# Where the low halves of four operands of the recurrence's branch are made

## The chip, the cores and the metric

One core of a Trainium2 chip runs the kernel. It has five engines that work beside each other: TensorE (PE in the profile, with its weight loads as PEld), VectorE (DVE), ScalarE (ACT), GpSimd (POOL) and SyncE (SP), and 16 DMA engines that serve queues which SP, ACT and POOL issue to. The metric is the device time of one execution in microseconds; lower is better. Everything is in float32.

## The reference

One decoder layer, sequence 1024, model width 1024. Cut to what matters:

```python
h    = rmsnorm(x, pre_g)
proj = h @ w_in           # z_ssm, xBC, dt, q, k, v, f, z_att, g_ssm, g_att
y_ssm = norm(ssd(conv_silu(xBC), softplus(dt)) * silu(z_ssm))   # the recurrence's branch
y_att = forgetting_attention(q, k, v, cumsum(log_sigmoid(f))) * silu(z_att)
p_ssm = y_ssm @ w_branch_ssm
p_att = y_att @ w_branch_att
merged = sigmoid(g_ssm) * p_ssm + sigmoid(g_att) * p_att
out = x + rmsnorm(merged @ w_out, post_g)
```

The recurrence is a chunked state-space scan of 16 heads; attention has 16 heads of 64 channels, is causal, and goes in blocks of 128 queries.

## The kernel before, in words

**Products in two pieces.** A float32 product is made from float32r matmuls: each operand is split into a high piece (a rounded copy, ACT) and a low piece (what the copy left over, DVE), and high·high, high·low and low·high are added in PSUM.

**Seven products for eight.** Every big matrix product (1024 x 1024 by two column blocks of 128) is a `Pair`, done by a Strassen-Winograd scheme with seven products of half size. The moving operand is cut into four blocks B11, B12, B21, B22 of 512 x 512, each four row tiles j = 0..3 of 128 x 512. The seven products need B11, B21, -B22 and the differences T1 = B12 - B11, T2 = B22 - T1, T3 = T2 - B11, T4 = T2 - B21. Each of the seven has a place in SBUF, a high tile and a low tile: x0 is B11, x1 is B21, x2 is -B22, x3 is T1, x4 is -T2, x5 is T3, x6 is T4 (so the profile's `x5l` is the low tile of T3, `x5h` the high one).

**The stream.** `Stream` lists the steps of all 47 pairs in order; a step is 12 matmuls of 128 x 512, done in two halves. TensorE's instructions stand in the order of the program, whatever the scheduler does with the other engines; instructions wrapped in `pin` keep the program's order on their engine too. All others are ordered by a planner that models the time. The first 24 pairs make the projections, then come 11 gate pairs (`late`), four for `w_branch_ssm` (their operand set is `ops_s`), four for `w_branch_att` (`ops_a`) and four for `w_out` (`ops_w`).

**Attention between the halves.** Attention runs over 8 pairs of heads with 6 groups each (m = 0..47). In each m the scores' matmuls go out, then some halves of the stream ("ahead"), then the transposes of the exponentials, then some more halves ("behind"), and the product with the values in the next m. DVE takes the scores with the bias and their minimum (L1505), ACT the exponentials (L1509), ACT or DVE the transposed blocks (L1548, L1546). POOL adds the causal mask to the bias tile (L1373).

**The operand set of the recurrence's branch.** `y_ssm` lies in DRAM as `ys_dram`. From the first m of attention on, `ops_s.differences` is worked off as a list (`stream.line`), one entry for each half of the stream: SP loads blocks (L227, L206), POOL subtracts (L211), POOL's queue stores T1..T4 in DRAM (L193, tensor `t_s`). The tile `x` has one buffer, the second operand is a `th` tile. `th` is a pool of four buffers of 128 x 512 (`small`), which serves the gates' results (L413 to L419, L629), `rb` (L1438), `st` (L1431) and more.

**The placing.** When the last gate pair has done its last step with an operand, that operand's tiles are opened for `ops_s`. `some`, called once in each half, issues loads (`fetch`, L263) of up to two row tiles and, some halves later, splits up to two: ACT makes the high tile from the raw one (L275, L278), DVE the low one (L276, L279). `ops_w` has been made otherwise in three operands: their low pieces are made early with the differences, kept in DRAM and loaded into the low tile (L261), the raw block is loaded into the high tile (L263), and only ACT's copy in place is left (L269).

Of the kernel before, what the change touches and what calls it, by code (L numbers as in the profile page):

```python
# [8 lines left out]
F32 = mybir.dt.float32  # L9
F32R = mybir.dt.float32r  # L10
BF16 = mybir.dt.bfloat16
AF = mybir.ActivationFunctionType
ALU = mybir.AluOpType
# [3 lines left out]
P = 128  # L17
# [3 lines left out]
KH = NK // 2  # L21
NT = T // P
HALF = 512
# [63 lines left out]
def hybrid_layer(ctx: ExitStack, tc, a, out):  # L87

    nc = tc.nc
# [43 lines left out]
    def pin(op):  # L133
        return tc.keep_in_program_order(op)

    def small(name="th"):
        return gp.tile([P, HALF], F32, tag="th", name=name)
# [21 lines left out]
    class Operands:  # L159
# [9 lines left out]
        def __init__(self, name, src, there=lambda k, h: True, order=lambda op: op, queue=nc.gpsimd):  # L169
            self.src, self.there, self.order, self.queue = src, there, order, queue  # L170
            self.copy = src
            self.tiles, self.left, self.made, self.at, self.step = {}, {}, set(), {}, 0
            self.lows = {}
            self.dram = {n: tc.dram_tile([KH, P, HALF], F32, name=f"{n}_{name}") for n in self.LESS}

        def __getitem__(self, name):
# [7 lines left out]
            return self.dram[name][j]  # L184

        def ready(self, name, j):
            if name in self.BLOCKS:
                r, h = self.BLOCKS[name]
                return self.there(KH * r + j, h)
            return (name, j) in self.made  # L190

        def store(self, name, j, t, cols=slice(0, HALF)):
            pin(self.queue.dma_start(self.dram[name][j][:, cols], t))  # L193
            if cols.stop == HALF:
                self.made.add((name, j))

        def differences(self, j, x, other, cols=slice(0, HALF), room=2, third=None):

            state = {}

            def fetch(name):
                state["y"] = other()
                self.order(nc.sync.dma_start(state["y"], self.block(name, j)[:, cols]))  # L206

            def less(name, out_, a_, b_):
                def go():
                    t = {"x": state["x"], "y": state["y"]}  # L210
                    pin(nc.gpsimd.tensor_tensor(t[out_], t[a_], t[b_], ALU.subtract))  # L211
                    state["out"] = name, t[out_]

                return go

            def keep(following=None):
                def go():
                    name, t = state["out"]
                    self.store(name, j, t, cols)
                    if following:  # L220
                        fetch(following)

                return go

            def start():
                state["x"] = x()
                self.order(nc.sync.dma_start(state["x"], self.block("b12", j)[:, cols]))  # L227
                fetch("b11")

            def low(name):  # L230
                if third is None:
                    return

                def go():
                    t, y = third(), state["x" if name == "t4" else "y"]
                    if name == "b22":
                        pin(nc.scalar.activation(t.bitcast(F32R), y, AF.Copy, scale=-1.0))
                        pin(nc.vector.scalar_tensor_tensor(t.bitcast(F32R), y, -1.0, t, ALU.mult, ALU.subtract))
                    else:
                        pin(nc.scalar.activation(t.bitcast(F32R), y, AF.Copy))  # L240
                        pin(nc.vector.tensor_tensor(t.bitcast(F32R), y, t, ALU.subtract))
                    state["low"] = t

                yield go
                yield lambda: pin(self.queue.dma_start(self.lows[name][j][:, cols], state["low"]))

            wait = (None,) * room
            yield from (start, *wait, less("t1", "x", "x", "y"), keep("b22"), *wait)
            yield from (*low("b22"), less("t2", "x", "y", "x"), keep("b11"), *wait)
            yield from (less("t3", "y", "x", "y"), keep(), *low("t3"), *wait[1:], lambda: fetch("b21"), *wait)  # L250
            yield from (less("t4", "x", "x", "y"), keep(), *low("t4"))
# [5 lines left out]
        def fetch(self, name, j):  # L257
            block = name.strip("-")
            raw = self.tiles[name][block not in self.lows][:, j, :].bitcast(F32)
            if block in self.lows:  # L260
                nc.sync.dma_start(self.tiles[name][1][:, j, :].bitcast(F32), self.lows[block][j])  # L261
            r, c = self.BLOCKS.get(block, (0, 0))
            nc.sync.dma_start(raw, self.copy(KH * r + j, c) if block in self.BLOCKS else self.dram[block][j])  # L263

        def split(self, name, j, raw=None):
            h, l = (t[:, j, :] for t in self.tiles[name])
            if name.strip("-") in self.lows:

                pin(nc.scalar.activation(h, h.bitcast(F32), AF.Copy, scale=-1.0 if name[0] == "-" else 1.0))  # L269
                self.left[name].remove(j)  # L270
                return
            if raw is None:
                raw = l.bitcast(F32)
            if name[0] == "-":
                pin(nc.scalar.activation(h, raw, AF.Copy, scale=-1.0))  # L275
                pin(nc.vector.scalar_tensor_tensor(l, raw, -1.0, h, ALU.mult, ALU.subtract))  # L276
            else:
                pin(nc.scalar.activation(h, raw, AF.Copy))  # L278
                pin(nc.vector.tensor_tensor(l, raw, h, ALU.subtract))  # L279
            self.left[name].remove(j)  # L280
# [39 lines left out]
    class Pair:  # L320
# [78 lines left out]
        def keep(self, ps):  # L399
            s = wp.tile([P, HALF], F32, tag="s", bufs=3, name="s")  # L400
            with tc.high_priority():
                nc.scalar.activation(s, ps, AF.Copy)  # L402
            return s
# [57 lines left out]
    class Stream:  # L461
# [73 lines left out]
        def half(self):  # L535
            if self.run is None:
                if self.at == len(self.steps):
                    return False
                p, which = self.steps[self.at]
                if which == 7 and p.ops is ops_a and "merged" not in fin:  # L540
                    return False
                if p.ops is ops_a and not all(p.ops.ready(OPERAND[which].strip("-"), j) for j in range(KH)):
                    return False
                self.ahead(False)
                for ops in self.building:
                    ops.some(OPERAND[which])
                if self.at + 1 < len(self.steps):
                    after, then = self.steps[self.at + 1]
                    after.begin(then, after.sums + (after is p and which in (5, 7)), True)
                self.run = p.do(which)  # L550
                next(self.run)
            else:
                for _ in self.run:
                    pass
                self.run = None
                p, which = self.steps[self.at]
                if p in self.following:
                    ops = self.following[p]
                    if ops not in self.building:
                        self.building.append(ops)  # L560
                    ops.open(OPERAND[which])
                self.ahead(True)
                self.at += 1
            for ops in self.building:
                if self.held is None:
                    ops.some()
                else:
                    self.held.append(ops)
            for chores in (self.chores, self.line):
                if chores:  # L570
                    chore = chores.pop(0)
                    if chore:
                        chore()
            self.count += 1
            for w in self.waiting:
                w[0] -= 1
            for w in [w for w in self.waiting if w[0] <= 0]:
                self.waiting.remove(w)
                w[1]()
            return True  # L580
# [572 lines left out]
    ops_s = Operands("s", lambda k, h: ys_dram[k, :, half(h)])  # L1153
    ops_a = Operands("a", lambda k, h: ya_dram[k, :, half(h)], lambda k, h: (k, h) in attended)
    ops_w = Operands("w", lambda k, h: a["wo"][k * P : (k + 1) * P, half(h)], order=pin, queue=nc.sync)
    ops_w.lows = {n: tc.dram_tile([KH, P, HALF], F32, name=f"{n}_low") for n in ("t3", "t4", "b22")}
    ops_w.copy = lambda k, h: wo_dram[k, :, half(h)]

# [634 lines left out]
```

## Time and profile before

| what | us |
|---|---|
| median of 3 runs | 1278.0 |
| lowest and highest run | 1276.09, 1281.77 |
| profiled execution, its own time | 1273.87 |
| its span, first to last instruction | 1272.2 |
| busy: PE, DVE, ACT, POOL | 1246.1, 1012.9, 794.3, 319.3 |

The profile's times count from the first instruction of the span. `ops_s`'s differences are made from 683 to 898 us and placed from 908 to 976 us; attention goes on to about 1120 us. A view by stretches gives each engine's busy time within a stretch, with the number of its instructions in brackets. A row of a tile's view has shortest/median/longest duration in ns and the first and last start. A row of the waits has the total in us, the number of waits and the longest.

### The profile page before, as it was taken

How to read it: one execution, taken by the hardware profiler on the slowest of the kernel's cores; microseconds unless marked ns; L12 is line 12 of the kernel's file. 1: busy time of each engine (PE TensorE's matmuls, PEld its weight loads, DVE VectorE, ACT ScalarE, POOL GpSimd, SP SyncE). 2: the span in 40 equal slices, each digit the busy share in tenths (PEclk: the TensorE clock that was granted, in tenths of full speed). 3: DMA queues.
4: the chain of work that ended last, by engine and by line, in shares of the span. 5: the costliest groups of instructions: out<-in, count | busy, mean ns of one | idle time of the engine just before them, and what ended most of it. 6: DMA issues, size and time to landing. Idle time of an engine off the chain costs nothing.

```text
span 1272.2 us, 20822 instructions
## 1 busy us (share of the span) xinstructions
PE 1246.1 (98%) x6926; PEld 982.3 (77%) x6926; DVE 1012.9 (80%) x1994; ACT 794.3 (62%) x1737; POOL 319.3 (25%) x322
## 2 busy tenths in 40 slices
PE   5999999999999999999999999999999999999997
PEld 3678888888888888888887777777777777778886
DVE  7988886988888978997767676767789767886975
ACT  7745665556665765566555666666687666844753
POOL 4000440013400241115102124223112212356062
PEclk9999999999999999999999999999999999999999
DMA  8232452545436533744447576666687657766933
GB/s 300 69 120 76 146 162 88 191 152 182 138 101 215 175 127 117 219 146 140 142 149 252 162 228 212 217 214 218 232 286 263 224 184 249 249 221 199 364 110 105
DMA packets 152236, 233.56 MB, mean 184 GB/s; under 512 B 15201, under 2 KB 60737, under 8 KB 152129
## 3 DMA queue, kind: packets, MB, share of 16 engines
q1 hardware_dynamic: 136064, 196.08, 47.7%
q10 hardware_dynamic: 10560, 18.06, 3.8%
q0 software_dynamic: 5504, 18.09, 3.7%
q8 instruction: 54, 0.88, 0.3%
q14 instruction: 54, 0.43, 0.1%
HBM read 162.99 MB, written 72.34 MB: 185 GB/s over the span
## 4 chain that ended last, share of the span: by engine, by line
PE 86%; DMA 4%; DVE 4%; ACT 4%; issue 1%; SPq 0%; POOL 0%; DVEq 0%; ACTq 0%; POOLq 0%
PE pb L128 36%; PE pc L128 21%; PE pd L128 7%; PE av L128 5%; PE pt L131 5%; PE s L128 5%; PE yps L128 2%; PE st L128 1%; ACT ex L1509 1%; DMA xt<-in_x 1%; PE tr L131 1%; PE tr_v L131 1%; DMA v<-v_dram 1%; PE df L128 1%; DVE wop L350 1%
## 5 line engine op out<-in xcount | busy, mean ns | idle before, releaser
L350 DVE TENSOR_TENSOR wop<-sum,wop 128x512 fp32r<-128x512 f32 x180 | 140.2, 780 | 53.6 <-ACT wop L349 52.6
L349 ACT ACTIVATE wop<-sum 128x512 fp32r<-128x512 f32 x180 | 112.5, 626 | 109.0 <-DVE sum L355 52.4
L1509 ACT ACTIVATE ex<-ex,nm 128x512 f32<-128x512 f32 (+1 forms) x192 | 116.2, 606 | 71.9 <-DVE nm L1505 71.6
L402 ACT ACTIVATE s<-pb 128x512 f32<-128x512 f32 x144 | 85.3, 593 | 98.2 <-PE pb L128 96.2
L128 PE MATMUL pb<-x0h,wop 128*128 128x512 f32 x384 | 131.5, 399 | 0.0
L128 PE MATMUL pb<-x6h,wop 128*128 128x512 f32 x384 | 129.5, 395 | 1.3 <-ACT s L402 1.3
L128 PE MATMUL pb<-x5h,wop 128*128 128x512 f32 x384 | 130.1, 396 | 0.7 <-ACT s L402 0.7
L350 DVE TENSOR_TENSOR wop<-raw,wop 128x512 fp32r<-128x512 f32 x144 | 105.4, 733 | 31.8 <-ACT wop L349 31.5
L128 PE MATMUL pc<-x3h,wop 128*128 128x512 f32 x384 | 129.8, 396 | 0.5 <-DVE ot L419 0.4
L128 PE MATMUL pc<-x2h,wop 128*128 128x512 f32 x384 | 130.2, 397 | 0.0
L128 PE MATMUL pb<-x4h,wop 128*128 128x512 f32 x384 | 129.1, 395 | 0.0
L1505 DVE CUSTOM_DVE_ANT_0 ex<-s,fb 128x512 f32<-128x512 f32 (+1 forms) x192 | 96.8, 552 | 20.0 <-PE s L128 14.8
L349 ACT ACTIVATE wop<-raw 128x512 fp32r<-128x512 f32 x144 | 89.7, 623 | 14.7 <-PE pd L128 6.1
L128 PE MATMUL pd<-x1h,wop 128*128 128x512 f32 x288 | 96.3, 394 | 0.0
L128 PEld LDWEIGHTS pb<-x6h,wop 128*128 128x128 f32 x384 | 72.1, 188 | 18.6 <-issue 2.0
L128 PEld LDWEIGHTS pb<-x5h,wop 128*128 128x128 f32 x384 | 72.1, 188 | 18.4 <-issue 2.0
L128 PEld LDWEIGHTS pb<-x0h,wop 128*128 128x128 f32 x384 | 72.6, 189 | 17.6 <-issue 2.9
L128 PEld LDWEIGHTS pc<-x3h,wop 128*128 128x128 f32 x384 | 72.1, 188 | 17.7 <-issue 1.5
L128 PEld LDWEIGHTS pc<-x2h,wop 128*128 128x128 f32 x384 | 72.1, 188 | 17.4 <-issue 2.4
L128 PEld LDWEIGHTS pb<-x4h,wop 128*128 128x128 f32 x384 | 72.1, 188 | 16.7 <-issue 1.9
L211 POOL TENSOR_TENSOR wd<-wd 128x256 f32<-128x256 f32 x32 | 32.4, 1011 | 205.0 <-DMA wd<-in_wo 135.0
L131 PE MATMUL pt<-ident,ex 128*128 128x128 f32 x576 | 75.1, 273 | 2.0 <-ACT ex L1509 1.4
(318 smaller groups left out, 2993.6 us busy)
## 6 DMA issues: line engine op xcount, KB each, us to landing
raw<-in_wu SPq DMA_DIRECT2D x128, 256.0 KB
csb<-cs_dram SPq DMA_DIRECT2D x32, 256.0 KB
q<-q_dram SPq DMA_DIRECT2D x32, 256.0 KB
k<-k_dram SPq DMA_DIRECT2D x16, 512.0 KB
fb<-f_dram SPq DMA_DIRECT2D x16, 512.0 KB
rb<-st_dram SPq DMA_DIRECT2D x48, 128.0 KB
wd<-in_wo SPq DMA_DIRECT2D x40, 128.0 KB
xt<-in_x SPq DMA_DIRECT2D x8, 512.0 KB
```

The source lines that it names most:

```text
L128: return tc.keep_in_program_order(nc.tensor.matmul(*args, **kw))
L131: return tc.keep_in_program_order(nc.tensor.transpose(out_, in_, idn))
L211: pin(nc.gpsimd.tensor_tensor(t[out_], t[a_], t[b_], ALU.subtract))
L349: nc.scalar.activation(op[:, 0], src, AF.Copy)
L350: nc.vector.tensor_tensor(op[:, 1], src, op[:, 0], ALU.subtract)
L402: nc.scalar.activation(s, ps, AF.Copy)
L1505: nc.vector.tensor_tensor_reduce(o, s[e][:, 0:w], fb[hp, h][:, e, 0:w], 1.0, 3.0e38, ALU.add, ALU.min, nm)
L1509: pin(nc.scalar.activation(o, o, AF.Exp, scale=-1.0, bias=nm, accum_out=hd.at(hd.sm, i, h, e)))
```

## The change

Four of the seven operands of `ops_s`, namely T1, T3, T4 and B22, get their low pieces while the differences are made. `lower` takes a `th` buffer, lets ACT write the high piece into it and DVE turn it into the low piece (for B22 with the sign turned), and stores it on POOL's queue in a DRAM tensor of its own. ACT's and DVE's instruction and the store are pinned. The list of `differences` has 20 entries for a row tile where it had 19: `part` makes the piece one half after the stored difference, and T2's difference comes in the same half as B22's piece, behind it. An operand of these four counts as made only when its low piece has been issued. In the placing, `fetch` then loads two blocks for a row tile in place of one, and `split` is ACT's copy in place. T2, B11 and B21 stay as they are, and so do `ops_a` and `ops_w`.

```diff
             self.tiles, self.left, self.made, self.at, self.step = {}, {}, set(), {}, 0
-            self.lows = {}
+            self.lows, self.late = {}, ()
...
         def ready(self, name, j):
-            if name in self.BLOCKS:
+            if name in self.BLOCKS and name not in self.late:
...
-            if cols.stop == HALF:
+            if cols.stop == HALF and name not in self.late:
                 self.made.add((name, j))
+
+        def lower(self, name, j, t):
+
+            s = small()
+            pin(nc.scalar.activation(s.bitcast(F32R), t, AF.Copy, scale=-1.0 if name == "b22" else 1.0))
+            if name == "b22":
+                pin(nc.vector.scalar_tensor_tensor(s.bitcast(F32R), t, -1.0, s, ALU.mult, ALU.subtract))
+            else:
+                pin(nc.vector.tensor_tensor(s.bitcast(F32R), t, s, ALU.subtract))
+            pin(self.queue.dma_start(self.lows[name][j], s))
+            self.made.add((name, j))
...
             wait = (None,) * room
+            if self.late:
+                part = lambda name, t: lambda: self.lower(name, j, state[t])
+                behind = lambda *fns: lambda: [fn() for fn in fns]
+                yield from (start, *wait, less("t1", "x", "x", "y"), keep("b22"), part("t1", "x"), None)
+                yield from (behind(part("b22", "y"), less("t2", "x", "y", "x")), keep("b11"), *wait)
+                yield from (less("t3", "y", "x", "y"), keep(), part("t3", "y"), lambda: fetch("b21"), *wait)
+                yield from (less("t4", "x", "x", "y"), keep(), part("t4", "x"))
+                return
             yield from (start, *wait, less("t1", "x", "x", "y"), keep("b22"), *wait)
...
         def split(self, name, j, raw=None):
             h, l = (t[:, j, :] for t in self.tiles[name])
-            if name.strip("-") in self.lows:
+            if raw is None and name.strip("-") in self.lows:
...
+    ops_s.late = ("t1", "t3", "t4", "b22")
+    ops_s.lows = {n: tc.dram_tile([KH, P, HALF], F32, name=f"{n}_low_s") for n in ops_s.late}
```

## The prediction

> **What bounds the kernel now.** I read the page first, then the view by stretches over attention, then the waits in two stretches, and last the rows of the tiles that the change touches.
>
> ```profile
> span 1272.2 us, 20822 instructions
> ...
> PE 1246.1 (98%) x6926; PEld 982.3 (77%) x6926; DVE 1012.9 (80%) x1994; ACT 794.3 (62%) x1737; POOL 319.3 (25%) x322
> ...
> PE 86%; DMA 4%; DVE 4%; ACT 4%; issue 1%; SPq 0%; POOL 0%; DVEq 0%; ACTq 0%; POOLq 0%
> ```
>
> TensorE is busy for 98% of the span and makes 86% of the chain that ended last. The change adds and removes no matmul and leaves their order alone. So time can only come from stretches in which TensorE stands or is stretched, and only be lost by making it stand. Here are the two stretches that matter, the making of the differences (683 to 910 us) and the placing (910 to 980), and then pieces of 20 us.
>
> ```profile
> core 0: us, PE busy (x) PEld busy (x) DVE busy (x) ACT busy (x) POOL busy (x), PEclk, DMA share, GB/s
> 683.00:910.00 227.00, 226.34 (x1532) 172.13 (x1530) 160.85 (x433) 148.71 (x378) 62.87 (x77) 1.00 0.62 203
> 910.00:980.00 70.00, 68.24 (x445) 49.92 (x444) 60.35 (x151) 54.34 (x133) 12.51 (x19) 1.00 0.82 281
> ```
>
> ```profile
> 860.00:880.00 20.00, 20.00 (x133) 15.30 (x132) 15.99 (x38) 13.38 (x32) 8.97 (x12) 1.00 0.67 212
> ...
> 900.00:920.00 20.00, 20.00 (x141) 14.93 (x137) 14.64 (x42) 13.38 (x33) 1.85 (x3) 1.00 0.72 247
> 920.00:940.00 20.00, 19.90 (x143) 15.12 (x137) 17.17 (x48) 15.26 (x39) 4.58 (x7) 1.00 0.79 271
> 940.00:960.00 20.00, 18.73 (x113) 12.95 (x109) 18.63 (x41) 16.71 (x41) 2.71 (x5) 1.00 0.90 312
> 960.00:980.00 20.00, 19.62 (x128) 14.61 (x125) 18.25 (x46) 15.88 (x40) 4.68 (x6) 1.00 0.69 228
> 980.00:1000.00 20.00, 20.00 (x141) 15.47 (x140) 14.48 (x44) 12.51 (x35) 6.57 (x8) 1.00 0.57 181
> ```
>
> The granted clock is 1.00 throughout. TensorE stands 0.66 us in the whole making of the differences. In the placing it stands 1.76 us, 1.27 of them from 940 to 960, where DVE is busy for 18.63 of 20 us and ACT for 16.71. The waits of that piece name the chain, scores to DVE's minimum to ACT's exponential to the transposes:
>
> ```profile
> ACT ex L1509 <- DVE nm L1505: 3.3, 3, 1.4
> ...
> PEld pt L131 <- ACT ex L1509: 1.2, 1, 1.2
> ...
> PE pt L131 <- ACT ex L1509: 0.9, 1, 0.9
> ```
>
> **What the change takes away.** Sixteen DVE subtractions leave the placing (four operands, four row tiles). In the crowded piece DVE's timeline has six of them, among the minima that the exponentials wait for:
>
> ```profile
> 950.08 0.68 DVE L279 TENSOR_TENSOR x5l<-x5l,x5h 128x512 fp32r<-128x512 f32 x1
> ...
> 951.63 0.68 DVE L279 TENSOR_TENSOR x5l<-x5l,x5h 128x512 fp32r<-128x512 f32 x1
> ...
> 955.61 1.28 DVE L279 TENSOR_TENSOR x5l<-x5l,x5h 128x512 fp32r<-128x512 f32 x2
> 956.81 1.29 DVE L279 TENSOR_TENSOR x3l<-x3l,x3h 128x512 fp32r<-128x512 f32 x2
> ```
>
> Six at 0.68 us are 4.1 us: DVE's load from 940 to 960 falls from 18.63 to 14.5, that of 980 to 1000, where TensorE does not stand at all. ACT keeps its copies, so 16.71 of 20 stays there. The least that can be gained, if DVE was the cause, is the visible standing, 1.76 us. The most comes from the weight loads: the pieces 860, 900, 920 and 980 hold 15.2 us of them on average, 940 to 960 is short of that by 2.25 and 960 to 980 by 0.6, together 2.85 us of loads or 2.85 / 15.2 x 20 = 3.75 us of work (part of it may be another mixture of matmuls). I take **-2.5**, near the middle, because ACT's share stays.
>
> **What it adds beside attention.** Per piece one ACT copy, one DVE subtraction, one store on POOL's queue; sixteen of each. These are the rows for them:
>
> ```profile
> L278 ACT ACTIVATE x5h<-x5l x7: 615/621/622, 946.5 to 1103.8; 128x512 fp32r<-128x512 f32 x7
> ```
>
> ```profile
> L350 DVE TENSOR_TENSOR wop<-raw,wop 128x512 fp32r<-128x512 f32 x23 | 18.5, 804 | 13.7 <-ACT wop L349 13.7
> ```
>
> ```profile
> L193 POOL DMA_DIRECT2D t_s<-x x12: 542/559/559, 691.1 to 898.4; - x12
> ...
> DMA to landing us min/median/max: 2.3/3.0/8.1
> ```
>
> ACT: 16 x 0.62 = 9.9 us. DVE: the same shape with both sources in SBUF has a mean of 804 ns between 683 and 910 us, so 16 x 0.80 = 12.9 us. POOL: 16 x 0.56 = 9.0 us. Over 227 us that is +1.1 us of DVE and +0.9 of ACT in each 20. The fullest piece shown, 860 to 880, goes to 17.1 for DVE and 14.3 for ACT. The nearest row is 920 to 940, with 17.17 and 15.26: TensorE stood 0.10 us there. So the load alone costs from 0 to 0.1 in each of 11 pieces, 1.1 us, and the average piece is well below that row: **+0.5**.
>
> The 0.80 us deserve a look, since the same subtraction takes 0.68 in the placing. POOL's own differences stretch as well:
>
> ```profile
> L1373 POOL TENSOR_TENSOR fb<-fb,far 64x256 f32<-64x256 f32 x34 | 25.5, 749 | 54.1 <-DVE nm L1505 39.2 <-ACT ex L1509 13.5
> L211 POOL TENSOR_TENSOR x<-x,th 128x512 f32<-128x512 f32 x8 | 10.7, 1343 | 9.4 <-DMA th<-ys_dram 9.0
> ...
> L211 POOL TENSOR_TENSOR th<-x,th 128x512 f32<-128x512 f32 x4 | 6.4, 1589 | 0.3
> ```
>
> The Trainium skill, page "SBUF — State Buffer", section "SBUF: two separate sides", says that a DVE instruction with two sources in SBUF and a GpSimd instruction that reads SBUF exclude each other for a whole instruction. That speaks against this change, since it moves two-source subtractions to where POOL is 28% busy (62.87 of 227) from where it is 18% busy (12.51 of 70). The trace agrees in kind, by 804 ns against 0.68 us; by the rule each collision would cost DVE up to a whole POOL instruction, 1.6 us, and 28% of 16 would be 7.2 us of DVE where the means give 1.9. DVE would then gain 1.6 us in each 20 in place of 1.1, and the sum would be some 0.5 us higher.
>
> **The waits that it adds.** ACT's copy is pinned: it waits for POOL's difference, and the exponentials of the following scores stand behind it on ACT. It comes two halves after the difference. A half lasts 2.92 us, from the first T1 to the last T4, 71 entries of the list apart:
>
> ```profile
> L211 POOL TENSOR_TENSOR x<-x,th x8: 1278/1287/1718, 689.6 to 896.8; 128x512 f32<-128x512 f32 x8
> ```
>
> (896.8 - 689.6) / 71 = 2.92, and the difference takes 1.3, so it is done as a rule. DVE's subtraction waits at most ACT's 0.6 us. The store waits on POOL for DVE; behind it stand the next difference, the masks (L1373) and attention's stores. POOL is idle for 164 of the 227 us, and TensorE has no wait there that names it: 0 at best; at worst 16 x 1.4 (a copy and a subtraction) = 22 us, if every mask came that much late. I take 0, by that absence.
>
> The copy also needs one of the four `th` buffers. Their shortage shows already, in four waits that name the last user of such a buffer and not a source:
>
> ```profile
> DVE th L419 <- DMA gs_dram<-th: 1.7, 1, 1.7
> ...
> ACT th L644 <- DMA za_dram<-th: 1.0, 1, 1.0
> ...
> ACT st L1431 <- POOL x L211: 0.9, 1, 0.9
> ...
> DVE th L419 <- DMA st_dram<-st: 0.8, 1, 0.8
> ```
>
> A piece holds its buffer through 0.62 + 0.80 + 0.56 and a landing of 3.0, 5 us; sixteen hold one for 80 us of 227 x 4. That is 9% more use, and if it doubles the waits, 4.4 us more of them stand on DVE and ACT. Of the standing of ACT and DVE little reaches TensorE:
>
> ```profile
> ACT ex L1509 <- DVE nm L1505: 33.2, 29, 3.0
> ...
> PEld s L128 <- ACT p L1548: 4.9, 14, 0.4
> ...
> PEld pt L131 <- ACT ex L1509: 1.4, 3, 0.5
> ...
> PE pt L131 <- ACT ex L1509: 0.5, 2, 0.3
> ```
>
> ACT's exponentials wait 33.2 us and TensorE for them 1.9. Bounds 0 and 4.4; I take **+1.5**, a third, since a pinned copy holds the exponentials themselves.
>
> **The placing, with more transfers.** Sixteen more loads of 128 x 512 x 4 bytes = 256 KB, at SP's 0.43 us each (row below) 6.8 us of SP, and 4.2 MB. From 910 to 980 the chip moves 281 GB/s x 70 us = 19.7 MB at a share of 0.82; 23.9 MB would be 341 GB/s, a share of 1.00 (281 / 0.82 = 343). It fits with nothing to spare. The loads come early: T4's raw tiles are asked for from 950.7 and split from 963.2.
>
> ```profile
> L278 ACT ACTIVATE x6h<-x6l x7: 615/617/625, 963.2 to 1124.0; 128x512 fp32r<-128x512 f32 x7
> ...
> L263 SPq DMA_DIRECT2D x6l<-t_s x4: 320/426/528, 950.7 to 953.6; - x4
> ```
>
> Twelve us of lead against some 4 us of delay (worked out below): **+0.5**, from bounds of 0 and 4. The list ends four halves later, about 12 us, so the last piece is issued near 912 us and T4 is loaded from 950: nothing is late for that reason. The planner lays out all unpinned instructions anew; by the spread of the three runs (1276.1 to 1281.8) that is taken at **+0.5**, bounds -2 and +2.
>
> **Sum:** -2.5 + 0.5 + 0 + 1.5 + 0.5 + 0.5 = +0.5 us on the profiled execution's 1273.87 (its span 1272.2 and 1.7 around it), so 1274.4. The runs' median lies 4.1 above that execution, which gives **1278.5**. With the ends of the terms (POOL's 22 us left to the first rival, which is of its kind) this case reaches from 1272.2 to 1287.7; both ends need every term at its end, so its likely part is 1274 to 1285.
>
> **Rivals.**
> *Buffers block the exponentials (slower).* A pinned copy that finds all four `th` buffers held stands on ACT until a store has landed, 3.0 to 8.1 us, and holds the exponentials. A half of 2.92 us covers TensorE; what is left is 0.1 to 5.2, on average 2.6 us for each blocked copy. If five of sixteen are blocked it costs 13 in place of the 1.5: +12, 1290. It passes 0.5% from the third copy on. For it: the four waits above. Against it: their longest is 1.7.
> *The transfers become the bound.* From 940 to 960 the chip moved 312 GB/s at 0.90, that is 6.2 MB; with the eight low tiles of T1 and T4 it is 8.3 MB, 24 us at 312 / 0.90 = 347 GB/s. Everything in the queue lands 4 us later, attention's loads too; if TensorE takes all of it, 1282. The page "DMA: Bandwidth & Descriptors" of the Trainium skill, section "Specifications", gives a core some 358 GB/s of HBM; by that the 8.3 MB take 23.3 us and the delay is 3.3, and the trace's 347 agrees.
> *Relief alone.* All added work is covered and the whole 3.75 us come back: 1274.3. For it: 0.66 us of standing in 227.
> *It does not do what it says*, pieces not ready in time and the old way taken: the 38 us of lead leave it hardly a chance; 1278.
>
> **How the numbers follow.** Forecast 0.50, buffers 0.20, transfers 0.10, relief 0.18, nothing 0.02. What a measurement of this kernel can tell from no change is about 0.5%, 6.4 us: below 1271.6 or above 1284.4. Faster: only the tails of relief and forecast, 0.04. Slower: 0.18 of buffers, 0.03 of transfers, 0.04 of the forecast's upper end, 0.25. Within: 0.71. The range 1273 to 1290 leaves out the lower tails and half of the buffers' case.
>
> **What would show it.** Right: from 940 to 980 DVE falls by some 11 us, TensorE stands less than 0.5 us there, low tiles are loaded from the new tensors; from 683 to 920 DVE rises by 11 to 13 us and TensorE's standing stays under 3 us. Wrong: ACT's new copy waits for a landing or for POOL, the transposes wait for ACT's exponentials by more than 5 us between 683 and 920, or TensorE waits for a DMA after 930. A gain over 4 us would mean that the pieces after 980 or before 683 were planned otherwise.

## The result, and the profile after

| | before | after |
|---|---|---|
| median, us | 1277.7 (6 runs) | 1290.45 (6 runs) |
| lowest and highest run | 1276.09, 1281.77 | 1287.23, 1296.43 |
| profiled execution, its span | 1273.87, 1272.2 | 1289.37, 1287.7 |

The ratio is 1.01, with an interval of [1.0073, 1.0127]: the change costs 12.7 us, 1%. The forecast was 1278.5 with a range up to 1290, so the result lies just outside it, where the first rival (1290) had been put. The page of after, to be read against that of before:

```profile
span 1287.7 us, 20914 instructions
...
PE 1249.7 (97%) x6926; PEld 981.4 (76%) x6926; DVE 1011.8 (79%) x1994; ACT 803.8 (62%) x1753; POOL 324.6 (25%) x338
...
PE 74%; DMA 9%; DVE 7%; ACT 4%; issue 4%; SPq 1%; POOL 0%; ACTq 0%; DVEq 0%; POOLq 0%
```

Busy times hardly moved: ACT has the 9.5 us of copies, DVE's total is the same to 1.1 us. What moved is the chain: TensorE's share falls from 86 to 74%, and DMA's and DVE's rise from 4 to 9 and 7%. TensorE now waits. The same matmuls show where. TensorE's order is equal in both kernels, so the scores of one m can be read off both timelines, first in before and then in after:

```profile
785.27 1.49 PE L128 MATMUL s<-k,q 64*128 64x512 f32 x12
...
863.92 1.66 PE L128 MATMUL s<-k,q 64*128 64x512 f32 x12
...
872.38 1.49 PE L128 MATMUL s<-k,q 64*128 64x512 f32 x12
...
917.76 1.66 PE L128 MATMUL s<-k,q 64*128 64x512 f32 x12
...
928.14 1.50 PE L128 MATMUL s<-k,q 64*128 64x512 f32 x12
...
985.02 1.50 PE L128 MATMUL s<-k,q 64*128 64x512 f32 x12
```

```profile
788.02 1.49 PE L128 MATMUL s<-k,q 64*128 64x512 f32 x12
...
870.24 1.66 PE L128 MATMUL s<-k,q 64*128 64x512 f32 x12
...
881.18 1.50 PE L128 MATMUL s<-k,q 64*128 64x512 f32 x12
...
928.10 1.66 PE L128 MATMUL s<-k,q 64*128 64x512 f32 x12
...
941.37 1.50 PE L128 MATMUL s<-k,q 64*128 64x512 f32 x12
...
998.81 1.50 PE L128 MATMUL s<-k,q 64*128 64x512 f32 x12
```

After is late by 2.8, 6.3, 8.8, 10.3, 13.2 and 13.8 us. Below, this difference is called the lag; the times that go with it are those of before. The loss falls where the pieces are made, and much of it in two steps, 2.5 us between 864 and 872 and 2.9 between 918 and 928. The stretches of after (same columns as in the prediction) say the same, with three rows of before behind them:

```profile
683.00:760.00 77.00, 76.19 (x513) 57.45 (x512) 56.93 (x150) 51.92 (x131) 18.60 (x25) 1.00 0.57 190
760.00:840.00 80.00, 78.37 (x529) 58.86 (x528) 55.77 (x152) 52.87 (x133) 26.35 (x36) 1.00 0.69 223
840.00:910.00 70.00, 67.54 (x437) 49.85 (x437) 49.13 (x123) 45.65 (x116) 19.90 (x26) 1.00 0.66 220
910.00:940.00 30.00, 27.45 (x178) 20.39 (x175) 22.84 (x59) 20.82 (x51) 7.73 (x10) 1.00 0.86 284
940.00:980.00 40.00, 39.90 (x269) 29.97 (x267) 29.86 (x81) 32.50 (x79) 7.61 (x13) 1.00 0.93 335
980.00:1040.00 60.00, 57.82 (x386) 43.18 (x384) 43.78 (x121) 37.72 (x99) 12.74 (x21) 1.00 0.74 243
```

```profile
760.00:840.00 80.00, 79.79 (x551) 60.37 (x548) 57.32 (x156) 51.81 (x132) 25.29 (x30) 1.00 0.66 225
840.00:910.00 70.00, 70.00 (x465) 53.90 (x465) 50.19 (x132) 46.26 (x116) 19.24 (x24) 1.00 0.63 203
...
940.00:980.00 40.00, 38.34 (x237) 27.57 (x232) 36.88 (x86) 32.58 (x80) 7.38 (x11) 1.00 0.79 270
```

TensorE stood 0 us from 840 to 910 before and stands 2.46 after; no engine is fuller there by more than 0.7 us, so it isn't load. In the placing after is some 13 us late, so its 940 to 980 holds what before does from about 927 to 967: DVE falls from 35.23 to 29.86 us there and TensorE's standing from 1.27 to 0.10, as was forecast. Over all the work that before does from 940 to 980 (953.2 to 993.8 in after) DVE falls from 36.88 to 28.23 us, but TensorE's standing rises from 1.66 to 2.28: the relief is given back at the end, where after stands 2.18 us from 980 to 1040.

Who is waited for, from 683 to 945 in after:

```profile
POOL t_low_s L205 <- DVE th L204: 90.7, 12, 18.0
...
DVE th L204 <- ACT th L200: 8.1, 7, 2.2
...
DVE ex L1526 <- POOL fb L1394: 3.6, 1, 3.6
...
DVE th L438 <- DMA ga_dram<-th: 2.0, 1, 2.0
...
DVE th L436 <- DMA st_dram<-st: 1.6, 1, 1.6
...
ACT th L200 <- DMA gs_dram<-th: 2.0, 2, 1.2
...
PEld pt L131 <- ACT ex L1530: 7.7, 13, 1.4
```

(Lines have moved by some 20: L200 is the new copy, L204 the new subtraction, L205 the new store, L1526 the minimum, L1530 the exponentials, L436 and L438 the gates' results, L1394 the mask.) Three waits on DVE and ACT end with the landing of a store from a `th` or `st` tile, which is no source of the waiting instruction: it waits for the buffer. The two steps of the lag are two of them, in the timeline:

```profile
872.49 0.69 DVE L436 TENSOR_TENSOR th<-pc,s 128x512 f32<-128x512 f32 x1 [1.56 <-DMA st_dram<-st]
...
874.77 0.68 DVE L1526 CUSTOM_DVE_ANT_0 ex<-s,fb 128x512 f32<-128x512 f32 x1
...
931.77 0.69 DVE L438 TENSOR_TENSOR th<-s,pc 128x512 f32<-128x512 f32 x1 [1.97 <-DMA ga_dram<-th]
...
932.37 0.68 DVE L1526 CUSTOM_DVE_ANT_0 ex<-s,fb 128x512 f32<-128x512 f32 x1
...
934.44 0.44 PE L131 MATMUL pt<-ident,ex 128*128 128x128 f32 x2 [0.93 <-ACT ex L1530]
...
936.15 0.33 PE L131 MATMUL pt<-ident,ex 128*128 128x128 f32 x1 [1.27 <-DVE nm L1526]
```

Pieces' stores were issued at 868.96 and 928.45, and by the tile's view they take 3.8 us to land (median). Before they have landed, DVE's gate result takes the next `th` buffer and finds none free. It stands for 1.56 and 1.97 us at the head of DVE's queue, the minima behind it start late, then ACT's exponentials, and in the second case TensorE stands at the transposes for 0.93 and 1.27 us. The buffer that it gets isn't the piece's own. The piece holds one of four, and so that of `st`, or of an earlier gate's store, still on its way, is now needed back.

### The profile page after: what moved, and what is told of

The parts are those of the page before. It is cut to its first block, busy times and chain, and to the rows that moved or that the text cites. A ratio compares the mean times of both kernels' runs of the same rounds, so it can differ in the third digit from the quotient of the medians.

```text
span 1287.7 us, 20914 instructions
## 1 busy us (share of the span) xinstructions
PE 1249.7 (97%) x6926; PEld 981.4 (76%) x6926; DVE 1011.8 (79%) x1994; ACT 803.8 (62%) x1753; POOL 324.6 (25%) x338
## 4 chain that ended last, share of the span: by engine, by line
PE 74%; DMA 9%; DVE 7%; ACT 4%; issue 4%; SPq 1%; POOL 0%; ACTq 0%; DVEq 0%; POOLq 0%
PE pb L128 31%; PE pc L128 18%; PE pd L128 7%; PE av L128 4%; PE pt L131 4%; PE s L128 4%; PE yps L128 2%; DVE wop L369 2%; DMA raw<-in_wu 2%; DMA rb<-st_dram 1%; ACT ex L1530 1%; DMA x6l<-t_low_s 1%; PE st L128 1%; DMA xt<-in_x 1%; DVE sum L374 1%
## 5 line engine op out<-in xcount | busy, mean ns | idle before, releaser
L1530 ACT ACTIVATE ex<-ex,nm 128x512 f32<-128x512 f32 (+1 forms) x192 | 116.2, 606 | 79.1 <-DVE nm L1526 78.3
L1526 DVE CUSTOM_DVE_ANT_0 ex<-s,fb 128x512 f32<-128x512 f32 (+1 forms) x192 | 96.7, 552 | 19.5 <-PE s L128 10.7
```

The lines of the kernel that those rows point to most:

```text
L1526: nc.vector.tensor_tensor_reduce(o, s[e][:, 0:w], fb[hp, h][:, e, 0:w], 1.0, 3.0e38, ALU.add, ALU.min, nm)
L1530: pin(nc.scalar.activation(o, o, AF.Exp, scale=-1.0, bias=nm, accum_out=hd.at(hd.sm, i, h, e)))
```

## The experiments

The theory after reading: the buffers and the pinned order cost the time, not the work added. The rivals: the added load of ACT and DVE; the placing and its transfers; chance, since the first profile of before was a quick one. Ratios are to the kernel before on the same chip (its medians there: 1276.5 to 1277.5), with 95% intervals. The lag is worked out as above, over all matmuls near a time.

**What is the spread, and which half of the change costs?** Four kernels. `again` is the kernel before once more, without an edit.

> The kernel before, unchanged, for a second profile. Up to 683 us, ahead of the first instruction that the change moves, all kernels so far run 1.5 to 3.7 us later than the first profile of before. If that is how runs differ, this profile is 1 to 4 us later there too; if it comes from the change (more tensors in DRAM), it is within 0.5 us of the first profile. Time 1276 to 1280.

1276.05 us, ratio 0.9992 [0.9979, 1.0004]. The lag of this unchanged kernel is 1.3 us at 683 and 2.2 at the end. Up to 683 the lag of the other kernels is 0 to 3.7 us, and that is chance as well: in after, the instructions of DVE, ACT, POOL and SP come in the old order up to there. So the 2.4 us of lag that after has at 683, of 15.2 at the end, aren't the change's.

`make_only` makes and stores the pieces, and places by the old way (excerpt):

```diff
-            if block in self.lows:
+            if block in self.lows and block not in self.late:
```

> As the changed kernel while the differences are made (th buffer, ACT, DVE, store), but the placing is that of the kernel before: one load for a row tile, ACT's and DVE's split, the stored low pieces never read. Theory (making the pieces costs it): 1287 to 1294, the changed kernel's time plus the 2 us of relief that the placing loses. Rival (the placing's transfers cost it): 1277 to 1282.

1287.89, 1.0084 [1.0068, 1.01]: by the ratio making alone costs 10.7 us of the 12.7.

`raw_store` is the reverse: no piece is computed, the raw difference is stored in its place, and the placing is the new one.

```diff
-            s = small()
             ... (copy and subtraction go)
-            pin(self.queue.dma_start(self.lows[name][j], s))
+            pin(self.queue.dma_start(self.lows[name][j], t))
```

> As the changed kernel, but `lower` makes no low piece: it stores the raw difference (or raw B22) in the low piece's DRAM tensor, with no th buffer, no ACT copy and no DVE subtraction. The pinned store on POOL's queue and the whole new placing (two loads for a row tile, ACT's copy alone) stay. Theory (the loss of some 12 us comes from making the pieces beside attention): 1275 to 1281, the level of the kernel before or 2 us under it, because DVE is relieved in the placing. Rival (transfers, POOL's queue, the fuller placing): 1286 to 1292, like the changed kernel.

1279.72, 1.0019 [1.0005, 1.0033]. By the ratio the new placing, its sixteen stores and its transfers together cost 2.4 us; there is no net gain in it.

`tiny` is `make_only` with pieces of 32 columns: ACT, DVE and the stores do a sixteenth of the work, on the same buffers, in the same places of the program (excerpt).

```diff
+            c = slice(0, 32)
+            pin(nc.scalar.activation(s[:, c].bitcast(F32R), t[:, c], AF.Copy))
...
```

> As make_only, but each piece is 32 columns wide in place of 512: it takes a whole th buffer, ACT, DVE and the store at the same places, in the same order and with the same waits, with little time on the engines (some 0.1 us each) and little to store. Theory A (the four th buffers are short: the taking and holding of a buffer costs it): 1284 to 1292, near make_only. Theory B (the work of ACT and DVE between the scores' minima and the exponentials costs it): 1277 to 1281.

1287.6, 1.0086 [1.0069, 1.0103], as `make_only`. The work itself costs nothing that can be measured (the two intervals are some 2 us wide to each side); the load as a rival falls, and with it the question of what a subtraction beside POOL takes. In after the twelve subtractions for T1, T3 and T4 take 0.69 us in the mean, not the 0.80 that were reckoned with; the four for B22 take 0.81.

**Is it the number of pieces?** `half34` makes only those of T3 and T4, `half1b` only those of T1 and B22, eight each, in the manner of after.

```diff
-                part = lambda name, t: lambda: self.lower(name, j, state[t])
+                part = lambda name, t: lambda: self.lower(name, j, state[t]) if name in self.late else None
...
-    ops_s.late = ("t1", "t3", "t4", "b22")
+    ops_s.late = ("t3", "t4")
```

> As the changed kernel with T3 and T4 alone treated in the new way; T1 and B22 are placed as before, so 8 pieces in place of 16. If the cost goes with the number of pieces: half of it, with most of the placing's relief: 1281 to 1285. If the cost grows faster than the pieces (buffers that are only short when several are wanted at once): 1276 to 1280. If the order of the list costs it, whatever the number: 1286 to 1291.

> The other half of half34: T1 and B22 alone in the new way, th buffers and pins as in the changed kernel. If a few places cost it, those of T3's piece at 790 us and T4's at 925 us, these pieces cost little there: 1278 to 1283. If any use of a th buffer costs it, wherever it falls: 1286 to 1291, as half34. If the cost goes with the number of pieces: 1282 to 1285.

`half34`: 1290.01, 1.0101 [1.0083, 1.0119], all of the loss with half the pieces. `half1b`: 1278.89, 1.0017 [1.0006, 1.0027]. So it isn't a price per piece. It matters where a piece falls: in `half34` a piece of T3 stands ahead of the minima near 790 (below), and at 929.85, a few us behind a piece of T4, a gate's result has waited 1.8 us for a gate's store to land. In `half34`'s profiled execution up to 6.8 us come on top from TensorE's clock (last section); without them it would be some 6 us behind before.

**Buffer or order?** Two edits, each alone and both together. `ring_s` takes the piece's buffer from another ring, the three buffers `s` of 128 x 512 into which ACT copies products, and leaves the pins; `free` leaves the buffer and takes the pins off ACT's and DVE's instruction, while the store on POOL's queue keeps its pin; `ring_free` has the ring `s` and no pin at all, on the store neither. So the two don't make a clean pair. Edits of `ring_s`, of `free` (excerpt), and the line that `ring_free` has besides both:

```diff
-            s = small()
+            s = wp.tile([P, HALF], F32, tag="s", bufs=3, name="lw")
```

```diff
-                pin(nc.vector.tensor_tensor(s.bitcast(F32R), t, s, ALU.subtract))
+                (nc.vector.tensor_tensor(s.bitcast(F32R), t, s, ALU.subtract))
```

```diff
-            pin(self.queue.dma_start(self.lows[name][j], s))
+            (self.queue.dma_start(self.lows[name][j], s))
```

> As the changed kernel, but the piece's buffer comes from the ring of three buffers `s` (the copies of PSUM sums, seldom more than two in use), no longer from the four `th` buffers. Engines, pins, order of the list, stores and placing are as in the changed kernel. Theory A (the th buffers are short): 1276 to 1282. Theory B (the pinned instructions, waiting for POOL or for each other, hold up ACT and DVE): 1287 to 1292. If the s ring turns short in its place, ACT's copies of PSUM sums wait for a landing and the time stays over 1285 too; the waits tell the two apart.

> The changed kernel with the piece's three instructions unpinned: the planner may put ACT's copy, DVE's subtraction and the store where it likes; the th buffer stays. Theory A (th buffers: 7 us of the loss, pinned places: some 4): 1283 to 1288, the stands of DVE for a landing near 870 and 925 us stay. Theory B (the pins alone): 1276 to 1281.

> ring_s (the piece in the s ring) with the piece's three instructions unpinned. What ring_s has left of the loss, 5 us, lies at 768 us (the scores wait for a mask that stands behind the pinned store on POOL) and at 790 and 835 (DVE's minima behind the pinned subtraction). If the pins do that: 1276 to 1280. If it is the s ring or the planner's other choices: 1281 to 1285.

What is expected of `free` speaks of three instructions unpinned; its kernel unpins two.

| median, us (ratio) | all pinned | ACT and DVE not pinned |
|---|---|---|
| `th` buffer | 1290.45, after (1.01 [1.0073, 1.0127]) | 1286.77, `free`, store pinned (1.0091 [1.0067, 1.0115]) |
| ring `s` | 1282.7, `ring_s` (1.0045 [1.0029, 1.0061]) | 1278.46, `ring_free`, store not pinned (1.0017 [1.0003, 1.0031]) |

Each median less that of before on the same chip gives 12.7 and 10.3 us in the first row, 5.5 and 2.0 in the second. Down the left column the buffer alone is worth 7.2 us; down the right one the buffer and the store's pin together 8.3. Along the rows the pins are worth 2.4 and 3.5 us. Of these the 2.4 lie within the noise, since the intervals of after and `free` overlap almost wholly. Both edits change more than their name says, because the planner lays out anew: `ring_s` has some 9% of DVE's instructions between 683 and 950 us at another place in the order than after. What speaks for the buffer itself is the second step: in `ring_s` DVE has the piece's subtraction (925.06) and the gate's result (925.67) ahead of the minima (926.88) too, and the wait of 1.97 us is gone.

The waits of `free`, `ring_s` and, again with its own edit, `a_both` (below), from 683 to 945, one line of each:

```profile
DVE th L436 <- DMA t_low_s<-th: 3.7, 1, 3.7
```

```profile
ACT lw L200 <- DMA t_low_s<-lw: 2.3, 2, 1.8
```

```profile
ACT st L1452 <- DMA t_low_s<-lw: 3.5, 2, 1.8
```

In `free` the gate's result waits 3.7 us for the landing of a piece's own store: here the piece's buffer is the one needed. In `ring_s` the copy waits for the landing of an earlier piece, 2.3 us in two waits, and the two steps of the lag at 864 and 918 are gone. The lags in full, each less its value at 683:

| lag in us at | 800 | 864 | 900 | 945 | 957 | 1000 | 1240 |
|---|---|---|---|---|---|---|---|
| after | 2.2 | 3.9 | 7.9 | 10.8 | 9.2 | 11.4 | 12.8 |
| `ring_s` | 3.9 | 5.1 | 5.8 | 5.8 | 4.3 | 5.8 | 6.3 |
| `free` | 0.7 | 0.8 | 5.4 | 7.8 | 6.1 | 10.3 | 10.3 |
| `ring_free` | -0.6 | -0.3 | 0.7 | 0.7 | -0.5 | 1.8 | 1.7 |

The pins show by 800 (after and `ring_s` against the other two), the buffers from 864 to 945. Of the lag of `free` up to 1.7 us by 900 and as much again by 1000 are half clock (last section): its granted clock is 0.66 from 874 to 879 and 0.57 from 987 to 991. What the pins do is plain near 790. In before the minima follow the wop subtraction at once; in after, DVE does three more instructions first, the last of them the pinned subtraction. First before, then after:

```profile
787.90 0.68 DVE L350 TENSOR_TENSOR wop<-sum,wop 128x512 fp32r<-128x512 f32 x1
...
788.50 0.68 DVE L1505 CUSTOM_DVE_ANT_0 ex<-s,fb 128x512 f32<-128x512 f32 x1
```

```profile
789.64 0.68 DVE L369 TENSOR_TENSOR wop<-sum,wop 128x512 fp32r<-128x512 f32 x1
...
791.57 0.68 DVE L204 TENSOR_TENSOR th<-th 128x512 fp32r<-128x512 f32 x1
792.17 0.68 DVE L1526 CUSTOM_DVE_ANT_0 ex<-s,fb 128x512 f32<-128x512 f32 x1
```

The minima come 3.67 us later by the traces, 0.92 us of it more than the lag of 2.75. In `free` the piece's subtraction alone stands between the two (789.78, the minima at 790.38), and its lag at 800 is 0.7 in place of 2.2.

**Is POOL's queue the price of the pins?** `ring_sp` is `ring_s` with the store on SP's queue.

```diff
-            pin(self.queue.dma_start(self.lows[name][j], s))
+            pin(nc.sync.dma_start(self.lows[name][j], s))
```

> ring_s with the piece's store on SP's queue in place of POOL's, still pinned. If POOL's standing at the store makes the masks late: the jump at 768 us (1.2 us) goes and POOL's wait with it: 1280 to 1283. If SP's loads now stand behind the store instead: 1284 to 1290.

1285.79, 1.0069 [1.0046, 1.0092], against 1282.7 with the store on POOL. POOL no longer stands at the store, and it brings nothing. The pinned subtraction is still ahead of the minima near 790, behind an instruction of DVE that takes 2.09 us there, and TensorE stands for 2.57 us (row in the last section). `free` and `half1b` say the same of the store. In `free` it is still pinned, POOL stands at it for up to 16.8 us and masks come late on DVE (3.1 us in two waits), and yet the lag at 800 is small. `half1b` has POOL standing for up to 18.0 us and the same late mask as after (3.6 us), and loses 2.3 us in all. What ACT's pin and DVE's cost each wasn't separated.

**Can the shortage be mended elsewhere?** `st` is a small result of attention that takes a `th` buffer. `b_st` is the kernel before with `st` in the ring `s`; `a_both` has the piece and `st` there.

```diff
-                st = small("st")[0:8, 0:P]
+                st = wp.tile([P, HALF], F32, tag="s", bufs=3, name="st")[0:8, 0:P]
```

> The kernel before, with attention's `st` (8 x 128 in a buffer of 128 x 512) taken from the s ring in place of the th buffers. Theory A: th is short already (four waits, 4.4 us), so 1274 to 1278, the same or up to 3 us faster. Theory B: 1276 to 1280, no difference.

> As ring_s, with `st` from the s ring as well, so that th has one user less than in the kernel before. Theory A: the placing's relief of about 2 us is no longer given back at the next group's scores, where ACT stood for `st`'s buffer: 1273 to 1279. Theory B: 1287 to 1292.

`b_st`: 1275.49, 0.9987 [0.9974, 0.9999]. Three of the four waits on which the prediction rests are gone in it, 3.4 of 4.4 us, and it gains 1.7; the unchanged `again` came out 1.1 below as well, and the longest of the four, 1.7 us, isn't in its profile at all. So the shortage cost the kernel before next to nothing. `a_both`: 1295.24, 1.0137 [1.0111, 1.0163], the slowest of all. The line above names one cause: ACT now waits for a piece's landing at `st`, ahead of the transposed blocks, 3.5 us in two waits. The shortage had only moved into a ring of three. Up to 6.8 us more of its profiled execution are half clock (0.57 from 876 to 884, 0.66 from 900 to 905 and from 941 to 946); the rest of its loss wasn't followed.

**Can the change be saved?** `ring_free_sp_st` has all at once: ring `s`, no pins, the store on SP's queue, and `st` in the ring `s` from the second half of attention on.

```diff
+            (nc.sync.dma_start(self.lows[name][j], s))
...
+                st = (small("st") if self.hp < KH else wp.tile([P, HALF], F32, tag="s", bufs=3, name="st"))[0:8, 0:P]
```

> The piece in the s ring, unpinned, its store on SP's queue, and `st` from the s ring for the last four pairs of heads alone, where no pieces are made. If each of the named waits is gone, the making costs nothing and the placing keeps its 2 us, since `st` no longer waits for a th buffer at 976 us: 1273 to 1278. If one of them is not the cause: 1279 to 1284.

1277.04, 1.001 [0.9993, 1.0026]: as before, no faster. The loss can be taken away; the gain doesn't come.

**Where does the gain of the placing go?** `ring_free_make` is `ring_free` with the old placing, `ring_free_13` is `ring_free` for T1 and T3 alone, with half the transfers.

> ring_free while the pieces are made (s ring, unpinned, POOL's queue), with the placing of the kernel before; the low pieces are not read. If making the pieces so costs nothing, ring_free's remaining 2 us over before come from the new placing, which gives back more than its relief: 1275 to 1278. If the making still costs: 1279 to 1282.

> ring_free with T1 and T3 alone, whose splits fell in the crowded piece from 940 to 960 us; T4 and B22 are placed as before, so 8 more loads in place of 16. If the relief of 2 us was given back at 976 us because all the transfers of the placing run together (DMA share 1.0 there), it stays now: 1273 to 1277. If the relief is given back whatever the transfers: 1277 to 1280.

1277.92, 1.0012 [1.0001, 1.0023], and 1277.8, 1.0013 [1.0001, 1.0026]: both within the interval of `ring_free`. The lag tells more. Most kernels that place T3 in the new way gain between 945 and 957 (1.6 us in after, 1.5 in `ring_s`, 1.2 in `ring_free`, 1.6 in `ring_free_13`, 1.6 in `ring_free_sp_st`); `ring_free_make` gains 0.2. And they give back between 957 and 1000: 2.2, 1.5, 2.3, 1.0 and 1.1 us, `ring_free_make` nothing. (Up to 1.7 of `ring_free`'s 2.3 are half clock: its granted clock is 0.66 from 980 to 985.) `half34` is an exception: it gains 0.4 and gives nothing back. In after it shows in the scores that lie at 977 in before:

```profile
990.56 1.45 PE L128 MATMUL s<-k,q 64*128 64x512 f32 x6 [2.12 <-DVE p L1567]
```

TensorE is there sooner and waits for DVE's copy of transposed blocks (it waited 0.38 us for it before). Just ahead of that, DVE waits 1.60 us for ACT's `wop` copy (988.41), which ACT does after two copies of the placing (`x2h`, 986.72), and then ACT's `st` waits 0.89 us for a DVE instruction that is no source of it, it seems for its `th` buffer (989.78). No run takes these apart, so why DVE is late isn't settled. The transfers are a candidate, as `ring_free`'s stretch shows:

```profile
950.00:970.00 20.00, 20.00 (x134) 15.14 (x132) 13.78 (x38) 17.39 (x42) 4.03 (x7) 1.00 1.04 394
```

The share is 1.04. But `ring_free_13`, with half of the new loads, gives back 1.0 of its 1.6 as well, so they aren't shown to be the only cause.

## Why the prediction was wrong, step by step

- **The `th` buffers, +1.5 with bounds of 0 and 4.4: the step that failed.** It measures 7.2 us (after against `ring_s`), over the upper bound. I doubled the waits that the trace of before showed (1.7, 1.0, 0.9, 0.8) and let a third reach TensorE. But those waits had cost next to nothing (`b_st`), so they said nothing of the price of the next buffer; that depends on what stands behind the waiting instruction. The rival named the mechanism and 1290, at a chance of 0.20, though with ACT's copy as the one that is blocked. ACT's copy waited only 2.0 us for a buffer. It was DVE's gate result, with the minima behind it. That the rival's 1290 is the time measured is luck: its 13 us were blocked copies alone.
- **The pins, 0 "by that absence": wrong, some 2 to 4 us.** They are 2.4 and 3.5 by the medians, of which the second is at the edge of the noise, and 1.5 and 4.5 by the lag at 800. "At most ACT's 0.6 us" for the subtraction was 8.1 us in seven waits, up to 2.2, since the copy is queued on ACT too. The store stood at POOL's head for up to 18.0 us, and one mask came late, 3.6 us on DVE. But `half1b` has both and loses little, so it isn't the store. What cost was the place on DVE: the pinned subtraction fell ahead of the minima, and for that I had no term.
- **ACT's copy would find POOL's difference ready: right.** No wait of it names POOL.
- **The load, +0.5: right as far as can be told.** `tiny` bounds it at nothing measurable, and the stretched 0.80 us didn't come for twelve of the sixteen subtractions.
- **The relief, -2.5: right in place, too large, and not kept.** It is 1.2 to 1.6 us by the lag, under the 1.76 taken as the least, and DVE falls by 8.7 us in the same work where some 11 were forecast. 1.0 to 2.3 us come back by 1000. I asked what is late next only for the making, not for the placing: it was DVE's copy.
- **The transfers, +0.5:** I had 341 GB/s from 910 to 980, "nothing to spare". The share did reach 1.01 in after (970 to 990) and 1.04 in `ring_free`. What they cost is inside the 1.0 to 2.3 us and can't be told apart.
- **The profiled execution as a base:** 1273.87 was 3.8 below the median of six runs; going on from the median was right.

Of what was to show it wrong, "the transposes wait for ACT's exponentials by more than 5 us" came true: by the weight loads' waits 6.0 us up to 920, 7.7 up to 945, against 1.4 up to 920 in before.

## What to carry to other kernels

A step moved to where the engines have room is paid in what it holds and what it stands in front of, not in its busy time: count the buffers of the pool that it takes until its store has landed, list who takes the next one, and read what is queued behind that taker. A wait in the old trace that costs nothing is no price for the next one of its kind, so a safe bound for such a term is the longest landing times the takers. Pin as little as can be, and where a relief is forecast, ask which operand is late next at that very place.

## What the runs showed of the hardware

TensorE's clock can halve for a short time after a stand. `ring_sp`, stretches from 790 and, below, the first transposes after the stand:

```profile
790.00:794.00 4.00, 1.56 (x7) 0.94 (x5) 4.00 (x8) 0.80 (x4) 1.41 (x2) 1.00 0.80 301
794.00:798.00 4.00, 3.75 (x16) 2.65 (x17) 1.93 (x6) 3.85 (x12) 1.34 (x2) 0.57 0.30 79
798.00:802.00 4.00, 4.00 (x29) 2.63 (x29) 2.18 (x6) 1.57 (x5) 0.00 (x0) 1.00 0.36 87
```

```profile
794.13 2.11 PE L131 MATMUL pt<-ident,ex 128*128 128x128 f32 x8 [2.57 <-ACT ex L1530]
```

After 2.57 us without work the granted clock is 0.57 over 4 us: at 0.5 that is (1 - 0.57) x 4 / 0.5 = 3.4 us. Eight transposes take 2.11 us; in after, sixteen take 1.91 at 974.09. So a stand can be paid a second time, by up to 1.7 us. In `half34`'s profiled execution 13.6 us are at 0.5 (0.57 from 794 to 802, 0.66 from 934 to 939 and from 1129 to 1134), up to 6.8 us lost. In that of after there are none, though TensorE stands for 2.12 us at 988; so not every stand of this size is followed by one, and how long a stand must be isn't shown. But after's other runs have mean clocks of 0.994 to 0.997 where that one has 0.998, the slowest (1296.43) one of the two lowest. The mean of its six is 0.9957, that of `ring_s` 0.998, and the runs of before have means of 0.998 to 0.999. As an estimate, 0.003 of 1290 us, up to some 4 of the 12.7 us, are paid this way, and so up to 3 of the buffers' 7.2. The Trainium skill, page "TensorE: Matmul & The Clock Gate", section "HAM oscillation — how this bites in real kernels", gives the rule that no idle gap should exceed about 3.4 us; here the clock was at half after one of 2.57 us.

The 394 GB/s of `ring_free` at a share of 1.04 are more than the 347 that I had worked out as the most from before's rows, and than the 358 that the prediction cites from the Trainium skill, page "DMA: Bandwidth & Descriptors", section "Specifications".
